# Modulation by VectorE: a two-layer hybrid recurrent block in which all but the first third of adaLN leaves TensorE's matmuls

## The chip, the cores and the metric

One core of a Trainium2 chip runs the whole kernel in one launch. The metric is the device time in microseconds; lower is better.

## The reference

Two layers work on 256 context tokens and 1024 latent tokens of 1024 channels. Each layer has a mixing sub-layer with four head groups (HGRN2, mLSTM, retention, GLA) and a squared-ReLU MLP. What matters here is adaLN: per layer, two conditioning vectors (context and latent) are each multiplied by a 1024 x 6144 matrix, and the six pieces of the result shift, scale and gate the two sub-layers.

```python
for layer in range(DEPTH):
    mod_l = (jax.nn.silu(c) @ w_ada[layer] + b_ada[layer])[:, None, :]
    mod_c = (jax.nn.silu(c_ctx) @ w_ada[layer] + b_ada[layer])[None, None, :]
    sh1_l, sc1_l, g1_l, sh2_l, sc2_l, g2_l = jnp.split(mod_l, 6, axis=-1)
    ...
    pl = split_proj(modulate(xl, sh1_l, sc1_l) @ w_in[layer])
    ...
    xl = xl + g1_l * mixer_out(raw_l, pl, g_heads[layer], w_out[layer])
    ...
    xl = xl + g2_l * sq_relu_mlp(modulate(xl, sh2_l, sc2_l), w_ff1[layer], w_ff2[layer])
```

where `modulate(x, shift, scale)` is `rmsnorm(x) * (1.0 + scale) + shift`. In the last layer the context's rows are needed by the mixers alone: its gates and its MLP are computed for the latent tokens only.

## The kernel before

Activations lie channel by token: eight channel tiles of 128 partitions, 1280 tokens in blocks of 256, 512 and 512. Each dense product takes three TensorE passes over split operands (lines 295 to 297, `mm3`; 569, and 600 to 602 for the two projections with tokens on the partitions). Weights arrive by DMA on SP's queue, ScalarE makes the high part (L283) and VectorE the rest (L284).

**Modulation.** The weights of a layer are cut into three thirds r (of 2048 columns) and eight channel tiles k. `ada_unit(l, r, k)` loads four pieces of 128 x 512 (L373) and multiplies each by the conditioning, 32 columns of which two are used, into 32 partitions of one PSUM bank (L374); the bank sums over k. After eight units `ada_finish` copies the bank (L380), transposes it (L383), adds the bias (L387) and, for scales, one (L391). Layer 0's first third comes ahead of everything. Its other two thirds (16 units) stand among the mLSTM's work, through four buffers; layer 1's three thirds (24 units) stand in layer 0's MLP, one after each feature tile, through two buffers.

**Mixers.** For each head group a generator emits steps and yields an estimated cost; `Fill` emits parts of dense projections between the steps, in proportion to the cost. Where `fill.also` is set, every eighth part also emits one modulation unit. The order of the groups is GLA, HGRN2 (two pairs of heads), mLSTM (two), retention (two). A feature tile is twelve parts (three token blocks by four), a projection with tokens on the partitions twenty. HGRN2's steps are many small VectorE operations (L851 to L1006, the multiply of queries at L959, short products L924, L968, L987); the mLSTM's are at L1265 to L1345.

**MLP.** A turn takes two feature tiles: first product (24 matmuls for each of three token blocks into a bank, ScalarE at L471 and L472, VectorE at L473 and L474), after each tile a call of `filler()`, then the second product (six matmuls a bank), which VectorE adds into the residual (L494). Layer 0 has 16 turns over 1280 tokens.

The instructions are traced in this order; a list scheduler of the framework places them on the engines' queues by its own estimates, so an instruction may stand somewhat before or behind its traced place. Every engine runs its queue in order. Eight scratch buffers of 512 words (`tmps`) serve the MLP.

Of the kernel before, what the change touches and what calls it, by code (L numbers as in the profile page):

```python
# [15 lines left out]
NK = 8  # L16
# [8 lines left out]
# constant arrays, by shape alone: name -> words  # L25
CONSTS = [("ones32", 32), ("ones", 128), ("sel", 128), ("ident", 128), ("bones", 128), ("m64", 512), ("lmask", 160),
          ("mlmask", 256), ("hsel", 8), ("eps", 1)]
# small per-call parameters
PARAMS = [("cc", 256), ("bada", 96), ("gfin", 8), ("ghead", 16), ("lblog", 8), ("mlb", 4), ("glb", 4), ("rtl", 24)]

# T-layout feature tiles of w_in
# [22 lines left out]
class Buf:  # L54
    """n words a partition of a tile"""
# [19 lines left out]
class Heap:  # L75
    """Places buffers in a few tiles at trace time; reuse waits by the bytes touched."""
# [13 lines left out]
    def top(self, n):  # L90
        """from the end of the first tile, or of what is free"""
        i, o, m = max((f for f in self.free_list if f[2] >= n), key=lambda f: (f[0] == 0, f[0], f[1]))
        self.free_list.remove((i, o, m))
        if m > n:
            self.free_list.append((i, o, m - n))
        b = Buf(self.tiles[i].t, o + m - n, n)
        b.i = i
        return b

    def alloc(self, n, low=False):  # L100
        """next fit; first fit for what lives long"""
# [14 lines left out]
    def free_head(self, n, *bufs):  # L116
        """the first words of buffers that are done with"""
# [21 lines left out]
class Dense:  # L139
    """a projection: its weights in n halves, then the products in small parts"""  # L140
# [16 lines left out]
class Fill:  # L157
    """dense work in small parts, traced between the steps of a mixer; the next weights ahead"""
# [9 lines left out]
    def step(self):  # L168
        while self.q:
# [3 lines left out]
            for cost in gen:  # L173
                self.n += 1
                if self.also and self.n % 8 == 0:
                    for c in self.also:
                        cost += c
                        break
# [9 lines left out]
    def along(self, gen, ratio, mark=10 ** 9):  # L188
        """a mixer, with this work, up to the mark, between its steps"""
# [10 lines left out]
class K:  # L200
# [19 lines left out]
    # ------------------------------------------------------------------ memory  # L220
# [4 lines left out]
    def pool(self, name, sizes, side="left"):  # L225
        """a pool of one tile for each size"""
# [49 lines left out]
    # ------------------------------------------------------------------ dense helpers  # L276
    def whalf(self, src, b, slot, eng=None):
        """512 words a partition of weights as (hi, lo), [128, 512 / b, b]"""
# [9 lines left out]
    def wtile(self, src, ring, eng=None):  # L288
        """a [1024, 128] tile of weights: k -> (hi, lo)"""
# [12 lines left out]
    def logsig(self, out, z, tmp, bias=None, scale=1.0):  # L302
        """tmp = ln(1 + exp(-|z + bias|)); out = min(z, 0) - tmp when no bias"""
# [13 lines left out]
    # ------------------------------------------------------------------ small parameters  # L317
# [8 lines left out]
    def params2(self, tmp):  # L326
        """hgrn lower bounds of layer 1, retention log decays"""
# [22 lines left out]
        # retention: log sigmoid(z) = min(z, 0) - 2 atanh(u / (2 + u)), u = exp(-|z|)  # L350
# [17 lines left out]
    # ------------------------------------------------------------------ ada  # L368
# [24 lines left out]
    # ------------------------------------------------------------------ norms  # L393
    def rstd(self, tb, fast=False):
        """1 / rms by token on every partition; fast: the squares summed by matrix products only"""
# [30 lines left out]
    def norm_mod(self, l, tbs, sh, sc):  # L426
        """modulated norm, block by block; the next block's statistics ahead"""
# [27 lines left out]
    # ------------------------------------------------------------------ MLP  # L455
    def mlp(self, l, tbs, wring, aring, filler, first, after):
        """first: weights of the first tiles; after: what follows the last sum of a token block"""
# [50 lines left out]
    def final_block(self, tb):  # L508
        """the statistics of this block, then the norm of the block before it"""
# [5 lines left out]
    # ------------------------------------------------------------------ projections  # L515
# [7 lines left out]
    def reserve(self, S, names, keep):  # L523
        """buffers for later work, apart from what the work before it takes"""
# [7 lines left out]
    def denseT(self, tile, tbs, evac):  # L532
        """a tile of features by channels"""
# [14 lines left out]
    def denseVS(self, S, sp):  # L548
        """v of GLA with the decay inputs and the gates of mLSTM, 304 columns, in [token, channel] layout"""
# [27 lines left out]
    def turn(self, sp):  # L577
        """these inputs and gates in [channel, token] layout"""
# [1138 lines left out]
```

## Time and profile before

| | us |
|---|---|
| median of three runs | 3391.35 |
| lowest and highest | 3391.2, 3393.93 |
| span of the profiled execution | 3386.0 |
| TensorE busy in it (matmul) | 3308.9 |
| VectorE busy | 1957.8 |
| ScalarE busy | 1284.9 |

The span runs from the first to the last instruction; no other time is given for the profiled execution. Ends of matmuls are modelled, and a matmul's row lasts longer than its distance from the next, so starts are what to compare. On a line of the timeline "x4" merges neighbours; an fp32 product gives two records.

### The profile page before, as it was taken

How to read it: one execution, taken by the hardware profiler on the slowest of the kernel's cores; microseconds unless marked ns; L12 is line 12 of the kernel's file. 1: busy time of each engine (PE TensorE's matmuls, PEld its weight loads, DVE VectorE, ACT ScalarE, POOL GpSimd, SP SyncE). 2: the span in 40 equal slices, each digit the busy share in tenths (PEclk: the TensorE clock that was granted, in tenths of full speed). 3: DMA queues.
4: the chain of work that ended last, by engine and by line, in shares of the span. 5: the costliest groups of instructions: out<-in, count | busy, mean ns of one | idle time of the engine just before them, and what ended most of it. 6: DMA issues, size and time to landing. Idle time of an engine off the chain costs nothing.

```text
span 3386.0 us, 52462 instructions
## 1 busy us (share of the span) xinstructions
PE 3308.9 (98%) x21020; PEld 2620.0 (77%) x21020; DVE 1957.8 (58%) x3806; ACT 1284.9 (38%) x2670; POOL 10.9 (0%) x41
## 2 busy tenths in 40 slices
PE   7999999999999999999999999999999999999998
PEld 4787876778877777777788688788777788888887
DVE  4878675646554444444445567866765655555556
ACT  4667663435321121121121456865534322222223
POOL 0000000000000000000000000000000000000000
PEclk9999999999999999999999999999999999999999
DMA  5223336526122222222111212333315111111111
GB/s 201 69 65 105 109 101 185 154 68 204 34 80 72 60 69 72 60 66 74 54 38 38 84 38 69 118 109 117 104 61 162 50 45 50 50 50 50 47 47 66
DMA packets 165790, 278.83 MB, mean 82 GB/s; under 512 B 20072, under 2 KB 49416, under 8 KB 165288
## 3 DMA queue, kind: packets, MB, share of 16 engines
q1 hardware_dynamic: 164248, 273.65, 26.1%
q8 instruction: 165, 2.70, 0.3%
q10 hardware_dynamic: 1296, 1.81, 0.2%
q14 instruction: 81, 0.66, 0.1%
HBM read 229.75 MB, written 45.64 MB: 81 GB/s over the span
## 4 chain that ended last, share of the span: by engine, by line
PE 85%; DMA 6%; DVE 4%; ACT 3%; issue 1%; SPq 0%; ACTq 0%; DVEq 0%
PE psum L295 21%; PE psum L296 21%; PE psum L297 21%; PE psum L374 3%; DMA pc<-w_ada 2%; PE psum L799 2%; PE psum L569 2%; PE psum L600 2%; PE psum L602 1%; PE psum L601 1%; PE psum L786 1%; PE psum L802 1%; PE psum L987 1%; PE psum L674 1%; PE psum L1326 1%
## 5 line engine op out<-in xcount | busy, mean ns | idle before, releaser
L494 DVE SCALAR_TENSOR_TENSOR x<-psum,st,x 128x512 f32<-128x512 f32 (+1 forms) x648 | 442.2, 690 | 274.9 <-PE psum L297 274.2
L283 ACT ACTIVATE pc<-st 128x512 fp32r<-128x512 f32 x256 | 161.1, 632 | 878.9 <-PE psum L296 866.7
L295 PE MATMUL psum<-pc,pc 128*128 128x512 f32 (+1 forms) x1296 | 478.1, 369 | 0.0
L296 PE MATMUL psum<-pc,pc 128*128 128x512 f32 (+1 forms) x1296 | 475.8, 367 | 0.0
L295 PE MATMUL psum<-Hhi,pc 128*128 128x512 f32 (+1 forms) x1280 | 473.8, 370 | 1.5 <-ACT pc L283 1.5
L297 PE MATMUL psum<-pc,pc 128*128 128x512 f32 (+1 forms) x1296 | 475.3, 367 | 0.0
L296 PE MATMUL psum<-Hlo,pc 128*128 128x512 f32 (+1 forms) x1280 | 473.2, 370 | 0.0
L297 PE MATMUL psum<-Hhi,pc 128*128 128x512 f32 (+1 forms) x1280 | 470.9, 368 | 0.0
L295 PE MATMUL psum<-Hhi,pw 128*128 128x512 f32 (+1 forms) x1192 | 448.5, 376 | 0.7 <-ACT pw L283 0.7
L297 PE MATMUL psum<-Hhi,pw 128*128 128x512 f32 (+1 forms) x1192 | 443.9, 372 | 0.0
L296 PE MATMUL psum<-Hlo,pw 128*128 128x512 f32 (+1 forms) x1192 | 443.5, 372 | 0.0
L473 DVE TENSOR_TENSOR st<-st 128x256 f32<-128x256 f32 (+1 forms) x160 | 101.9, 638 | 397.1 <-ACT pc L472 396.9
L295 PEld LDWEIGHTS psum<-pc,pc 128*128 128x128 f32 x1296 | 244.2, 188 | 63.2 <-issue 12.0
L295 PEld LDWEIGHTS psum<-Hhi,pc 128*128 128x128 f32 x1280 | 241.3, 188 | 63.3 <-ACT pc L283 11.6
L297 PEld LDWEIGHTS psum<-pc,pc 128*128 128x128 f32 x1296 | 243.9, 188 | 53.0 <-issue 12.8
L296 PEld LDWEIGHTS psum<-Hlo,pc 128*128 128x128 f32 x1280 | 241.2, 188 | 49.8 <-issue 9.7
L284 DVE TENSOR_TENSOR pc<-st,pc 128x512 fp32r<-128x512 f32 x256 | 176.2, 690 | 173.6 <-ACT pc L283 151.5
L296 PEld LDWEIGHTS psum<-pc,pc 128*128 128x128 f32 x1296 | 244.3, 189 | 40.7 <-issue 2.1
L297 PEld LDWEIGHTS psum<-Hhi,pc 128*128 128x128 f32 x1280 | 241.1, 188 | 41.0 <-DVE pc L284 0.6
L295 PEld LDWEIGHTS psum<-Hhi,pw 128*128 128x128 f32 x1192 | 225.4, 189 | 51.0 <-issue 14.9
L297 PEld LDWEIGHTS psum<-Hhi,pw 128*128 128x128 f32 x1192 | 225.3, 189 | 41.0 <-issue 5.8
L296 PEld LDWEIGHTS psum<-Hlo,pw 128*128 128x128 f32 x1192 | 225.5, 189 | 37.6 <-issue 3.8
(418 smaller groups left out, 4810.7 us busy)
## 6 DMA issues: line engine op xcount, KB each, us to landing
st<-w_ff SPq DMA_DIRECT2D x256, 256.0 KB
st<-w_inT SPq DMA_DIRECT2D x96, 256.0 KB
pc<-w_ada SPq DMA_DIRECT2D x96, 256.0 KB
ph<-w_ada SPq DMA_DIRECT2D x64, 256.0 KB
st<-w_out SPq DMA_DIRECT2D x50, 256.0 KB
d_z<-st SPq DMA_DIRECT2D x40, 256.0 KB
ps<-w_ada SPq DMA_DIRECT2D x32, 256.0 KB
x<-xT SPq DMA_DIRECT2D x32, 256.0 KB
```

Of the source, the lines that this page charges most:

```text
L283: nc.scalar.activation(hi, raw, AF.Copy)
L284: (eng or nc.vector).tensor_tensor(lo, raw, F(hi), op=ALU.subtract)
L295: t.matmul(out, lhsT=w[0], rhs=m[0], start=first, stop=False)
L296: t.matmul(out, lhsT=w[0], rhs=m[1], start=False, stop=False)
L297: t.matmul(out, lhsT=w[1], rhs=m[0], start=False, stop=last)
L374: nc.tensor.matmul(self.bank(bank)[32 * g:32 * g + 32, :], lhsT=self.cc[:, k, :], rhs=w, start=(k == 0), stop=(k == NK - 1), tile_position ...
L473: nc.vector.tensor_tensor(r, r, r, op=ALU.mult)
L494: nc.vector.scalar_tensor_tensor(x, ps, self.mod[:, l, 40 + o, j:j + 1], x, op0=ALU.mult, op1=ALU.add)
L569: t.matmul(ps[:, 0:304], lhsT=h[a], rhs=u[b], start=(k + i == 0), stop=(k == NK - 1 and i == 2))
L600: t.matmul(ps[:, e, :], lhsT=h[0], rhs=u[0], start=(k == 0), stop=False)
L601: t.matmul(ps[:, e, :], lhsT=h[0], rhs=u[1], start=False, stop=False)
L799: nc.tensor.matmul(o, lhsT=ST[r0:r0 + kd, c, d, :], rhs=qd[d](c)[r0:r0 + kd, :], start=(j == 0), stop=False, tile_position=(r0, 0))
```

## The change

The first third of layer 0 stays as it is. All other thirds are made by a new function `ada_part`. It takes W columns at a time (256 in layer 0, 512 in layer 1). For each of the eight channel tiles it loads 128 x W weights and, for each conditioning that is wanted, VectorE multiplies them by the conditioning's value on each partition and adds them to an accumulator in SBUF. After the eighth, TensorE multiplies each 128 columns of an accumulator by one column of ones, which sums over partitions and leaves the result in the wanted layout; VectorE adds the bias. Layer 0 takes both conditionings. Layer 1 takes both for its first third and the latent one alone for the rest.

In layer 0 this now starts ahead of HGRN2 and goes on through the mixers: on parts 0, 2 and 4 of every five, one step (a load with its operations, or a sum), with no cost counted against the part; 144 steps in all. Its six buffers of 256 words are held from there to the mixers' end; the sums take a bank of the dense ring, which keeps its three banks in the mLSTM. In layer 0's MLP each call of `filler()` takes four steps (108 in all). Four scratch buffers leave the MLP's ring: two join the two load buffers, two are accumulators. Comments are removed as well; that part of the diff is left out.

```diff
@@ Fill.step
-                if self.also and self.n % 8 == 0:
-                    for c in self.also:
-                        cost += c
-                        break
+                if self.also and self.n % 5 in (0, 2, 4):
+                    next(self.also, None)
@@ new
+    def ada_part(self, l, r, toks, wring, tmp, acc, banks, W):
+        nc = self.nc
+        one = self.m64[:, 1:2]
+        nt, nb = len(toks), W // 128
+        for q in range(2048 // W):
+            g, h = divmod(q * W, 512)
+            A = [b(W) for b in acc[:nt]]
+            for k in range(NK):
+                w = wring.next()(W)
+                nc.sync.dma_start(w, self.io["w_ada"][l, r, k, :, g, h:h + W])
+                for i, j in enumerate(toks):
+                    c = self.cc[:, k, j:j + 1]
+                    if k == 0:
+                        nc.vector.tensor_scalar(A[i], w, c, None, op0=ALU.mult)
+                    else:
+                        nc.vector.scalar_tensor_tensor(A[i], w, c, A[i], op0=ALU.mult, op1=ALU.add)
+                yield
+            ps = self.bank(banks().next())
+            for i in range(nt):
+                for cb in range(nb):
+                    nc.tensor.matmul(ps[:, 2 * cb + i:2 * cb + i + 1], lhsT=A[i][:, 128 * cb:128 * cb + 128], rhs=one,
+                                     start=True, stop=True)
...
+            nc.vector.tensor_tensor(mo, v, bb, op=ALU.add)
...
+            yield
@@ mixers, ahead of HGRN2
+        ao = hp.alloc(1536, True) if l == 0 else None
+        if l == 0:
+            fill.also = ada([ao.sub(256 * i, 256) for i in range(6)], lambda: self.dbanks)
@@ mixers, mLSTM
-        ao = hp.alloc(2048) if l == 0 else None
-        if l == 0:
-            self.dbanks = Ring((0, 1))
...
-                fill.also = ada(p, Ring([ao.sub(512 * i, 512) for i in range(4)]))
...
-                for _ in fill.also:
-                    pass
@@ build
-                    b.ada_unit(0, i + 1, k, 2, ring)
-                    yield 860
-                b.ada_finish(0, i + 1, 2, 2, b.tD.next())
+            for r in (1, 2):
+                yield from b.ada_part(0, r, (0, 1), Ring(bufs[:4]), None, bufs[4:6], banks, 256)
...
-            b.ada_unit(1, r, k, st["bk"], fring)
-            if k == 7:
-                b.ada_finish(1, r, st["bk"], b.banks.next(), b.tmps.next())
+                yield from b.ada_part(1, r, (0, 1) if r == 0 else (1,), Ring(bufs[:4]), None, bufs[4:6], lambda: b.banks, 512)
+        tmps = b.tmps
+        gen = ada1(cs[nw:nw + nf] + tmps.items[4:])
+        def filler():
+            for _ in range(4):
+                next(gen, None)
+        if l == 0:
+            b.tmps = Ring(tmps.items[:4])
```

## Rows read from the trace of the kernel before

**Rows 1.** The page: span, then busy time, share and instructions by engine.
```profile
span 3386.0 us, 52462 instructions
...
PE 3308.9 (98%) x21020; PEld 2620.0 (77%) x21020; DVE 1957.8 (58%) x3806; ACT 1284.9 (38%) x2670; POOL 10.9 (0%) x41
```

**Rows 2.** The page: the chain that ended last, share of the span by line.
```profile
PE psum L295 21%; PE psum L296 21%; PE psum L297 21%; PE psum L374 3%; DMA pc<-w_ada 2%; PE psum L799 2%; PE psum L569 2%; PE psum L600 2%; PE psum L602 1%; PE psum L601 1%; PE psum L786 1%; PE psum L802 1%; PE psum L987 1%; PE psum L674 1%; PE psum L1326 1%
```

**Rows 3.** Timeline of TensorE, layer 0's MLP: first matmuls of turns 1, 12, 15.
```profile
995.77 0.28 PE L295 MATMUL psum<-Hhi,pc 128*128 128x256 f32 x1
...
1696.49 0.28 PE L295 MATMUL psum<-Hhi,pc 128*128 128x256 f32 x1
...
1862.21 0.28 PE L295 MATMUL psum<-Hhi,pc 128*128 128x256 f32 x1
```

**Rows 4.** Timeline of TensorE around a modulation unit in the MLP.
```profile
963.41 1.05 PE L374 MATMUL psum<-pc,st 128*32 128x512 f32 x4
964.40 0.39 PE L295 MATMUL psum<-pc,pc 128*128 128x256 f32 x1
...
968.52 1.04 PE L374 MATMUL psum<-pc,st 128*32 128x512 f32 x2 [1.17 <-DMA pc<-w_ada]
```

**Rows 5.** Waits of TensorE: us in total, times, longest.
```profile
PE psum L374 <- DMA pc<-w_ada: 13.4, 23, 1.2
...
PE psum L374 <- DMA ph<-w_ada: 2.0, 3, 1.0
```

**Rows 6.** Windows, L374 alone: length, then busy us (records) of PE and PEld.
```profile
515.00:810.00 295.00, 42.65 (x128) 5.80 (x128) 1.00 0.47 141
...
925.00:1680.00 755.00, 76.48 (x192) 10.20 (x192) 1.00 0.24 67
```

**Rows 7.** Windows: busy PE, PEld, DVE, ACT, POOL; clock, DMA share, GB/s.
```profile
515.00:675.00 160.00, 156.95 (x1044) 108.89 (x1042) 97.32 (x262) 64.18 (x182) 0.39 (x3) 1.00 0.59 176
236.00:515.00 279.00, 273.62 (x2779) 222.45 (x2778) 207.23 (x493) 180.93 (x420) 1.20 (x11) 1.00 0.33 104
...
2360.00:2480.00 120.00, 115.87 (x858) 94.03 (x859) 90.01 (x233) 61.75 (x175) 0.31 (x2) 1.00 0.34 105
929.00:1697.00 768.00, 753.83 (x3669) 579.96 (x3668) 347.31 (x553) 147.09 (x258) 0.00 (x0) 1.00 0.23 67
```

**Rows 8.** Timeline of TensorE around a block of L924.
```profile
178.31 0.73 PE L924 MATMUL psum<-st,px 128*128 128x4 f32 x6
178.90 0.48 PE L297 MATMUL psum<-Hhi,pw 128*128 128x512 f32 x1
179.21 0.39 PE L295 MATMUL psum<-Hhi,pw 128*128 128x512 f32 x1
```

**Rows 9.** VectorE by line and form, 236 to 515: busy us, mean ns.
```profile
L959 DVE SCALAR_TENSOR_TENSOR px<-px,st 128x512 f32<-128x512 f32 x40 | 30.0, 750 | 6.9 <-ACT px L957 4.4 <-DMA px<-d_z 1.8
...
L959 DVE SCALAR_TENSOR_TENSOR px<-px,st 128x256 f32<-128x256 f32 x20 | 9.7, 485 | 2.2 <-ACT px L957 1.1
```

**Rows 10.** Windows with VectorE nearly full (columns of rows 7).
```profile
2040.00:2060.00 20.00, 18.15 (x257) 13.71 (x255) 19.06 (x41) 14.84 (x30) 0.00 (x0) 1.00 0.26 93
2180.00:2200.00 20.00, 20.00 (x177) 15.05 (x176) 18.05 (x40) 17.51 (x37) 0.00 (x0) 1.00 0.38 120
```

**Rows 11.** TensorE by line and form, 236 to 515: one dense pass of three.
```profile
L295 PE MATMUL psum<-Hhi,pw 128*128 128x512 f32 x160 | 64.2, 401 | 0.0
L600 PE MATMUL psum<-pw,Hhi 128*128 128x256 f32 x123 | 36.2, 295 | 0.4 <-ACT ph L728 0.4
L295 PE MATMUL psum<-Hhi,pw 128*128 128x256 f32 x79 | 22.8, 288 | 0.0
```

**Rows 12.** Waits of SP's queue: us in total, times, longest.
```profile
SPq L282 <- DVE pc L284: 1284.7, 223, 16.7
```

**Rows 13.** The chain in order of time: one load in the MLP.
```profile
964.49 3.99 DMA pc<-w_ada
```

More of the change, by code (lines that the diff above doesn't have):

```diff
@@ L391, in ada_finish @@
             nc.vector.tensor_scalar(m, m, 1.0, None, op0=ALU.add)
+    def ada_part(self, l, r, toks, wring, tmp, acc, banks, W):
[20 more added lines that the diff above has]
+                                     start=True, stop=True)
+            o = 16 * r + nb * q
+            mo = self.mod[:, l, o:o + nb, toks[0]:toks[0] + nt]
+            bb = self.bada[:, l, o:o + nb].unsqueeze(2).to_broadcast([128, nb, nt])
+            v = ps[:, 0:2 * nb].rearrange("p (c j) -> p c j", j=2)[:, :, 0:nt]
+            nc.vector.tensor_tensor(mo, v, bb, op=ALU.add)
+            if (r == 0 and g >= 2) or (r == 2 and g < 2):
+                nc.vector.tensor_scalar(mo, mo, 1.0, None, op0=ALU.add)
+            yield
     def rstd(self, tb, fast=False):
@@ L1442, in mixers @@
         self.rt_setup()
-        ao = hp.alloc(2048) if l == 0 else None
-        if l == 0:
-            self.dbanks = Ring((0, 1))
         for p in range(2):
-            if l == 0:
-                fill.also = ada(p, Ring([ao.sub(512 * i, 512) for i in range(4)]))
             self.fetch(ml[p], "K", MLK + p, TBS)
@@ L1458, in mixers @@
             fill.until(m)
-            if l == 0:
-                for _ in fill.also:
-                    pass
-                fill.also = None
-        if l == 0:
-            hp.free(ao)
-            self.dbanks = Ring((0, 1, 2))
         hp.free(ml[0]["V65"], self.mlN_o, self.mlAE_o)
@@ L1476, in mixers @@
         fill.until(10 ** 9)
+        if l == 0:
+            for _ in fill.also:
+                pass
+            hp.free(ao)
         for x in self.mix_pools:
@@ L1566, in build, with ada @@
         b.mix_open(l)
-        def ada(i, ring, l=l):
-            if l == 0:
-                for k in range(NK):
-                    b.ada_unit(0, i + 1, k, 2, ring)
-                    yield 860
-                b.ada_finish(0, i + 1, 2, 2, b.tD.next())
+        def ada(bufs, banks):
+            for r in (1, 2):
+                yield from b.ada_part(0, r, (0, 1), Ring(bufs[:4]), None, bufs[4:6], banks, 256)
         b.mixers(l, ada)
@@ L1579, in build, with ada1 @@
         pc, cs = b.pool(f"pc{l}", [1024] * nw + [512] * nf + [NT] * (2 * na))
-        wring, fring = Ring(cs[:nw]), Ring(cs[nw:nw + nf])
+        wring = Ring(cs[:nw])
         aring = Ring(zip(cs[nw + nf::2], cs[nw + nf + 1::2]))
-        st = {"i": 0, "bk": None}
-        def filler(l=l, st=st):
-            if l == 1 or st["i"] >= 24:
-                return
-            r, k = divmod(st["i"], 8)
-            if k == 0:
-                st["bk"] = b.banks.next()
-                b.banks.items.remove(st["bk"])
-            b.ada_unit(1, r, k, st["bk"], fring)
-            if k == 7:
-                b.ada_finish(1, r, st["bk"], b.banks.next(), b.tmps.next())
-                b.banks.items.append(st["bk"])
-            st["i"] += 1
+        def ada1(bufs, l=l):
+            for r in range(3) if l == 0 else ():
+                yield from b.ada_part(1, r, (0, 1) if r == 0 else (1,), Ring(bufs[:4]), None, bufs[4:6], lambda: b.banks, 512)
[4 more added lines that the diff above has]
+                next(gen, None)
+        if l == 0:
+            b.tmps = Ring(tmps.items[:4])
         first = [b.wtile(io["w_ff1"][l, f], wring) for f in range(2)]
@@ L1604, in build @@
         b.mlp(l, tbs, wring, aring, filler, first, after)
+        b.tmps = tmps
         pc.release()
```

## The prediction

> **What bounds the kernel now.** I read the page first, then the chain that ended last, then TensorE's timeline by turns of the MLP, then the engines by stage. The page says that TensorE's matmul rows cover nearly the whole span and VectorE's a little over half [rows 1]. The chain carries the point: after the dense products (L295 to L297) it names L374, the modulation products, with 3%, and the loads of their weights with 2% [rows 2]. So the modulation lies on the path; but the chain splits time between a load and the products beside it, so I price it by turns.
>
> Layer 0's MLP runs 16 turns of two feature tiles. Turn 1 starts at 995.77, turn 12 at 1696.49: 700.72 us for eleven turns with modulation units, 63.70 each. From 1696.49 to 1862.21 three turns without units take 55.24 each [rows 3]. Nothing else differs between them, so a turn with two units costs 8.46 us more. Inside, a block of L374 holds TensorE 0.99 us (963.41 to 964.40), and the third group of a unit comes after an idle 1.17 us behind its load, since two buffers serve four loads [rows 4]. Named waits for loads sum to only 13.4 us in the MLP [rows 5]: most of the price is execution.
>
> The other two thirds of layer 0 stand among the mLSTM's products: 128 records, 42.65 us busy, against 192 records and 76.48 us in the MLP [rows 6]. TensorE is busy for 156.95 of 160 us there, VectorE for 97.32; in the HGRN2 stage before it VectorE is busy for 207.23 of 279 [rows 7]. The granted clock reads 1.00 in all these windows, so no term comes from it.
>
> **The change, part by part.**
>
> *Removed in the MLP.* Twelve turns by 8.46 are 101.6 us, the loads' waits included.
>
> *Added there on TensorE.* Each sum over partitions is an fp32 product of 128 weight columns with one moving column. The nearest row is L924 (128 weight columns, 2 or 4 moving): six records, three products, from 178.31 to 178.90, so 0.20 each, and the dense product behind them takes 0.31 in place of 0.23 [rows 8]. A block of four costs 0.87 us, of eight 1.66. Layer 1 has four blocks of eight (first third, both conditionings) and eight of four (the rest, latent alone): 13.6 us.
>
> *Added there on VectorE.* 64 + 64 multiply-adds of 512 columns. The row for that form is L959's 750 ns [rows 9]: 96 us. VectorE then has 347.31 + 96 = 443 us in a stretch of 768 - 84 = 684 us [rows 7], 65%. I cost this at nothing. The cover is PSUM: a filler call puts at most eight multiply-adds (6.0 us) ahead of an accumulation out of PSUM, and a bank in the second product is filled by six matmuls of 0.23 us (1.4 us), so eight banks hold some 8 us or more in mixed widths. Without that cover all 96 us could show. The scratch ring that shrinks from eight to four buffers turns once in four chains of 24 products (5.4 us each); an ordinary chain of ACT and VectorE work needs less. Nothing.
>
> *Removed in the mLSTM.* Lower bound the bare 42.65; upper bound the MLP's ratio of price to busy time, 101.6/76.48 = 1.33, which gives 56.7. I take 46, near the lower: waits for loads here are 2.0 us [rows 5], and many blocks stand between other fp32 products, where no dense product pays for the switch. TensorE must find other work to gain it: the same stage of layer 1 has no modulation and TensorE is busy 115.87 of 120 us there, 96.6% against 98.1% [rows 7]. I add 2 us for that.
>
> *Added in layer 0's mixers on TensorE.* 16 blocks of four: 13.9 us.
>
> *Waits of these 28 blocks.* Each waits for the last multiply-add of its sum. Nothing to 0.58 us each (13.4/23, what an L374 block waits for a load [rows 5]): 0 to 16 us. I take 4, as blocks can be planned behind dense work.
>
> *Added in layer 0's mixers on VectorE.* Two thirds by eight pieces by eight channel tiles by two conditionings: 256 operations of 256 columns, 485 ns [rows 9], 124 us. One in eight is a plain multiply, which I price the same. They ride on three of five dense parts, from HGRN2's start. Up to 515 us some 151 of the 250 remaining parts run: L295's 160 + 79 products at 24 a tile are 10 tiles of 12 parts, and L600's 123 at 4 a part are 31 [rows 11]. So 90 steps fall there, 80 of them loads with two operations: 78 us. VectorE in HGRN2 becomes 207 + 78 = 285 us in a stage that TensorE alone would make 279 + 9 = 288 long: 99%. In the mLSTM it is 97 + 25 in about 160 - 37 + 3 = 126 us, 97%. So VectorE runs out of slack here. Below, the additions fit into its 72 idle microseconds and cost nothing; above, it keeps every idle moment it has now and the stage becomes 207 + 78 + 72 = 357, 69 us longer than 288. Rows near that load: at 18.05 of 20 us VectorE busy TensorE still reads 20.00, at 19.06 it reads 18.15 [rows 10]. A VectorE held to 95% makes HGRN2 300 us, 12 longer; I take 12 for both stages.
>
> The width is the one doubtful choice. A 256-column operation costs 485 ns and two of them 0.97 us, against 0.75 for one of 512 [rows 9]. [...]
>
> *Buffers and banks.* The loads hold 1536 words a partition from HGRN2 on, where 2048 were held in the mLSTM alone, and the mLSTM's dense products get three banks in place of two. No row prices either. TensorE's idle time, 5.4 of 279 us and 3.1 of 160 [rows 7], bounds what the third bank can win, and the words are under one slot and a half of the five that hold weights, so I take nothing for both.
>
> *Loads.* The bytes are the same, but 128 loads of half the width take the place of 64, now waiting on VectorE where they waited on TensorE. SP already stands long behind weight loads (1284.7 us in total [rows 12]), and a w_ada load takes 3.99 us on the chain [rows 13]. What is queued behind a waiting load are weights, fetches and spills. With four buffers each load can go three steps ahead (554 us / 144 steps = 3.8 us a step, 11 us ahead), so I cost it at nothing; the price if that fails is a rival below.
>
> **Sum** on the profiled execution's span: 3386.0 - 101.6 + 13.6 - 46 + 13.9 + 2 + 4 + 12 = 3283.9. The median of the runs, 3391.35, stands 5.35 above the span; with that, 3289 us.
>
> **The rivals.**
>
> *VectorE sets the pace of layer 0's mixers.* The term of 12 goes towards its bound of 69. For it: 99% and 97% above. Against: the dense parts still fill TensorE while a mixer is late. Time 3305 to 3346, the middle 3320. Chance 0.22.
>
> *The mLSTM's products were cover, not path.* Then its 46 us come back as waits of TensorE and only the MLP gains: 3335. Against: TensorE's 98% there, and 96.6% in layer 1. Chance 0.08. [...]
>
> *The change doesn't lighten TensorE.* If a sum costs what an L374 block costs whatever its width (0.97), 128 sums cost 124 us in place of 27: about 3386, no change. Against: L924's rows. Chance 0.03.
>
> *The other side: loads late on VectorE's own queue.* In VectorE's queue a multiply-add that waits for its load holds every evacuation and mixer step behind it. Half of 3.99 us for each of 128 loads is 255 us, with VectorE full: 3540. It turns slower than before from 102/128 = 0.8 us a load. For it: SP's long stands. Against: three steps of lead. Chance 0.04.
>
> **How the numbers follow.** The forecast above has 0.60 (3263 to 3310), still better 0.03 (down to 3261, with 56.7 removed in the mLSTM, no waits and no loss to VectorE). The range, 3263 to 3335, holds the forecast's own and most of the first rival. About 0.2% (7 us) is what a measurement of this kernel can tell from no change; so faster 0.92, same 0.03, slower 0.05.
>
> **What would show it.** L374 is left in the first 35 us alone. Turns of layer 0's MLP are all near 55.2 us plus 1.1 for sums, with no TensorE idle time named by VectorE's accumulations. From 236 us on VectorE's share rises above 95% until the mLSTM's end, while TensorE's stays over 96%, and retention starts some 10 to 25 us sooner. Wrong: if TensorE's idle time in the mixers grows by tens of us with VectorE named; if VectorE's own waits name w_ada; or if the blocks of sums take much over 0.2 us a product.

## The result, and the profile after

The changed kernel takes 3307.68 us (median of four executions, 3300.05 to 3315.91); the kernel before took 3391.49 beside it. The ratio is 0.975, 95% interval [0.9733, 0.9767]: faster by 2.5%. The forecast was 3289, the range 3263 to 3335. The profiled execution is the fastest of the four: 3300.05, span 3298.2, against 3386.0 before.

The page after, answering to [rows 1]:

```profile
span 3298.2 us, 52930 instructions
...
PE 3215.6 (97%) x20936; PEld 2640.0 (80%) x20936; DVE 2121.8 (64%) x4218; ACT 1286.1 (39%) x2665; POOL 10.8 (0%) x41
```

TensorE lost 93 us of busy rows and VectorE gained 164. To see where the span fell, use the marks of [rows 3]. L293 to L295 are now the dense products, L413 the sums over partitions. Timeline of TensorE after:

```profile
307.47 0.40 PE L295 MATMUL psum<-Hhi,pw 128*128 128x512 f32 x1
312.41 1.08 PE L1018 MATMUL psum<-px 128*32 128x64 f32 x32 [4.55 <-DVE px L990]
318.07 1.08 PE L1018 MATMUL psum<-px 128*32 128x64 f32 x32 [4.58 <-DVE px L990]
321.50 0.79 PE L293 MATMUL psum<-Hhi,pw 128*128 128x512 f32 x1 [2.35 <-DVE st L741]
322.09 0.63 PE L294 MATMUL psum<-Hlo,pw 128*128 128x512 f32 x1
322.52 0.63 PE L295 MATMUL psum<-Hhi,pw 128*128 128x512 f32 x1
...
991.43 0.28 PE L293 MATMUL psum<-Hhi,pc 128*128 128x256 f32 x1
...
1005.21 1.84 PE L413 MATMUL psum<-st 128*128 128x1 f32 x16
1006.91 0.37 PE L293 MATMUL psum<-Hhi,pc 128*128 128x256 f32 x1
...
1219.57 0.28 PE L293 MATMUL psum<-Hhi,pc 128*128 128x256 f32 x1
...
1723.92 0.28 PE L293 MATMUL psum<-Hhi,pc 128*128 128x256 f32 x1
...
1779.16 0.28 PE L293 MATMUL psum<-Hhi,pc 128*128 128x256 f32 x1
```

Read the lower half first. Turn 1 of layer 0's MLP starts at 991.43 (995.77 before), turn 15 at 1779.16 (1862.21 before). So the span's 87.8 us divide into 4.3 ahead of turn 1, 78.7 in turns 1 to 14, and 4.75 behind. Nearly all of it came in the MLP's turns; the 4.75 lie in layer 1, which the change doesn't touch, and are within chance (see ahead of experiment 1). The four turns from 991.43 to 1219.57 take 57.04 each, one without modulation still 55.24 (1723.92 to 1779.16). The 4.3 ahead of turn 1 hold turn 0's own gain, so the mixers, from which the forecast expected 16 us, gave nothing that one execution can tell. The upper half shows why: TensorE stood still for 4.55, 4.58 and 2.35 us, with VectorE named, and the products behind follow each other by 0.43 us (322.09 to 322.52) where the same form took 0.23 (1003.62 to 1003.85 in the same timeline).

The engines after, by stretch (columns of rows 7): HGRN2 from its start to the mLSTM's first product at 545.3 (before: 236 to 515), the mLSTM, the MLP's turns, and then, in slices of 20 us, the part of HGRN2 in which TensorE stands still most (called the hole below):

```profile
236.00:545.00 309.00, 282.08 (x2772) 227.75 (x2771) 260.90 (x655) 181.17 (x412) 1.28 (x12) 0.95 0.41 125
545.00:687.00 142.00, 140.19 (x1041) 118.57 (x1040) 111.97 (x316) 67.48 (x193) 0.24 (x2) 1.00 0.43 126
991.00:1697.00 706.00, 706.00 (x3738) 609.51 (x3737) 409.99 (x674) 145.17 (x257) 0.00 (x0) 1.00 0.23 70
...
290.00:310.00 20.00, 17.41 (x190) 13.21 (x188) 18.93 (x50) 16.45 (x43) 0.00 (x0) 1.00 0.26 84
310.00:330.00 20.00, 10.66 (x126) 8.64 (x127) 17.40 (x40) 7.41 (x14) 0.00 (x0) 0.66 0.26 86
```

HGRN2's stretch grew from 279 to 309 us. That length is not a loss by itself, since other dense parts run in it: run 9 below has no hole, and its mLSTM's first product still comes at 530.5. The idle time is: TensorE idles 26.9 us of it where it idled 5.4 [rows 7], and its granted clock has a mean of 0.95 where it was 1.00: between 310 and 330 it is 0.66, where the timeline has the idle times. In windows of half a microsecond it reads 1.00 up to 311.5, 0.50 from 312 to 325 (the lower level below) and 1.00 again from 325.5. VectorE is busy for 260.90 of 309, 84%, and not the 99% that the prediction worked out. The MLP's stretch shows the opposite: TensorE without any idle time.

What VectorE did while TensorE waited until 312.41 (timeline of VectorE after; L990 is L959 of before):

```profile
305.25 1.67 DVE L408 SCALAR_TENSOR_TENSOR ph<-ph,st 128x256 f32<-128x256 f32 x4
306.84 0.69 DVE L310 SCALAR_TENSOR_TENSOR st<-psum,st 128x512 f32<-128x512 f32 x1
...
308.78 0.68 DVE L722 TENSOR_TENSOR st<-st,psum 128x512 f32<-128x512 f32 x1
309.74 0.75 DVE L990 SCALAR_TENSOR_TENSOR px<-px,st 128x512 f32<-128x512 f32 x1 [0.28 <-ACT px L988]
310.40 1.22 DVE L731 TENSOR_TENSOR_SCAN st<-st 128x512 f32<-128x512 f32 x1
311.54 0.72 DVE L990 SCALAR_TENSOR_TENSOR px<-px,st 128x512 f32<-128x512 f32 x1
```

Four multiply-adds (1.59 us from start to start) and three operations of the dense work stand in the queue among the mixer's steps; the L990 that TensorE needs ends at 312.26. From 305.25 to 312.26 VectorE is idle for 0.28 us in all. No single operation is to blame. Each delays all that stands behind it in the queue, and TensorE's next product in its own queue needs this one result.

Two views answer the doubts about loads and sums. The multiply-adds themselves (operation of L408 in the mixers, count, ns, idle time ahead), and all of VectorE's waits for these loads in the mixers; then TensorE's waits from 236 to 900:

```profile
L408 DVE SCALAR_TENSOR_TENSOR ph<-ph,st 128x256 f32<-128x256 f32 x224 | 99.7, 479 | 0.2 <-DMA ph<-w_ada 0.2
```

```profile
PE psum L1018 <- DVE px L990: 10.1, 5, 4.6
...
PE psum L413 <- DVE ph L408: 3.5, 1, 3.5
```

VectorE waited 0.2 us for loads in 224 operations, and TensorE 3.5 us, once, for the last multiply-add of a sum. There is a wait the other way too, which the prediction doesn't have: the plain multiply that begins a sum (L406) waited 4.2 us, in two times, until TensorE had read the two accumulators. Its waits end at 714.7 and 740.3, not in the hole.

### The profile page after: what moved, and what is told of

Its sections match the earlier page's. It is cut to its first block, busy times and chain, and to the rows that moved or that the text cites. A ratio compares the mean times of both kernels' runs of the same rounds, so it can differ in the third digit from the quotient of the medians.

```text
span 3298.2 us, 52930 instructions
## 1 busy us (share of the span) xinstructions
PE 3215.6 (97%) x20936; PEld 2640.0 (80%) x20936; DVE 2121.8 (64%) x4218; ACT 1286.1 (39%) x2665; POOL 10.8 (0%) x41
## 4 chain that ended last, share of the span: by engine, by line
PE 88%; DVE 5%; DMA 3%; ACT 3%; issue 1%; SPq 0%; DVEq 0%; ACTq 0%
PE psum L293 23%; PE psum L294 23%; PE psum L295 23%; PE psum L830 2%; PE psum L600 2%; PE psum L631 2%; PE psum L633 2%; PE psum L632 1%; PE psum L817 1%; PE psum L833 1%; PE psum L1018 1%; PE psum L705 1%; PE psum L1357 1%; PE psum L413 1%; DVE px L990 1%
## 5 line engine op out<-in xcount | busy, mean ns | idle before, releaser
L293 PE MATMUL psum<-pc,pc 128*128 128x512 f32 (+1 forms) x1296 | 475.8, 367 | 0.0
L295 PE MATMUL psum<-pc,pc 128*128 128x512 f32 (+1 forms) x1296 | 473.8, 366 | 0.0
L293 PE MATMUL psum<-Hhi,pc 128*128 128x512 f32 (+1 forms) x1280 | 471.9, 369 | 1.7 <-ACT pc L281 1.5
L295 PE MATMUL psum<-Hhi,pc 128*128 128x512 f32 (+1 forms) x1280 | 470.5, 368 | 0.0
L293 PE MATMUL psum<-Hhi,pw 128*128 128x512 f32 (+1 forms) x1192 | 451.0, 379 | 5.7 <-ACT pw L281 2.5
L295 PE MATMUL psum<-Hhi,pw 128*128 128x512 f32 (+1 forms) x1192 | 445.2, 374 | 0.0
L293 PEld LDWEIGHTS psum<-pc,pc 128*128 128x128 f32 x1296 | 244.4, 189 | 43.8 <-DVE x L525 1.3
L295 PEld LDWEIGHTS psum<-pc,pc 128*128 128x128 f32 x1296 | 244.0, 188 | 43.0 <-issue 2.7
L293 PEld LDWEIGHTS psum<-Hhi,pc 128*128 128x128 f32 x1280 | 241.2, 189 | 43.5 <-ACT pc L281 2.4
L295 PEld LDWEIGHTS psum<-Hhi,pc 128*128 128x128 f32 x1280 | 241.1, 188 | 40.9 <-DVE pc L282 0.6
L293 PEld LDWEIGHTS psum<-Hhi,pw 128*128 128x128 f32 x1192 | 226.7, 190 | 51.4 <-issue 10.1
L295 PEld LDWEIGHTS psum<-Hhi,pw 128*128 128x128 f32 x1192 | 226.2, 190 | 37.6 <-issue 2.1
```

The costliest lines, as they stand in the source:

```text
L293: t.matmul(out, lhsT=w[0], rhs=m[0], start=first, stop=False)
L295: t.matmul(out, lhsT=w[1], rhs=m[0], start=False, stop=last)
```

## The experiments

"T1" below is the start of turn 1 in the profiled execution: it holds the mixers and turn 0 and nothing that follows. It is 995.77 before, 991.43 after.

How much of a T1 is chance? Layer 1's mixers, from turn 15 to the first product of layer 1's MLP, tell. No edit reaches them, and the counts of instructions agree to a record or two; yet this stretch takes from 799.57 us (run 11) to 809.66 (run 9), 803.17 after and 807.83 before. Run 11, then run 9, windows (columns of rows 7):

```profile
1778.81:2578.38 799.57, 780.51 (x6136) 625.93 (x6134) 542.35 (x1156) 441.32 (x947) 8.73 (x21) 1.00 0.29 93
...
1752.16:2561.82 809.66, 788.12 (x6136) 632.21 (x6134) 542.13 (x1156) 441.33 (x947) 8.75 (x21) 0.99 0.29 92
```

VectorE and ScalarE are busy as long in both; the granted clock is not the same (last section). So a difference of some us between two T1 is not read below, and up to 10 us may be chance; the medians and their intervals come first.

**1. The MLP's part alone.** Layer 0's other thirds stay L374 products in the mLSTM; the MLP is as changed.

```diff
-                if self.also and self.n % 5 in (0, 2, 4):
-                    next(self.also, None)
+                if self.also and self.n % 8 == 0:
+                    for c in self.also:
...
```

> The change in layer 0's MLP alone; layer 0's second and third thirds stay on TensorE in the mLSTM as before. By the profile after, turns of the MLP fell from 63.70 to 57.04 and 56.14 us, some 85 us over the twelve turns, and that is nearly all of the gain. So if the mixers' part of the change is worth nothing net (all theories of why agree on this), this kernel takes 3306 us, the same as the changed one within its spread. If the mixers' part had won what was forecast for it (16 us), it takes 3324 us. Its granted clock should be that of the kernel before, 0.996.

3298.14 us, ratio 0.9733 [0.9715, 0.9751], T1 987.22. The MLP is worth 2.7%, some 90 us; the mixers' part is worth nothing that can be measured (the intervals overlap, and the 4.2 us by which T1 is earlier without it may be chance). The T1 of this kernel stands 8.55 ahead of before, near the 8.46 of turn 0's products.

**2. The latent conditioning alone in layer 0** (the context's gates, shifts and scales are not computed: they take the latent ones).

```diff
-                yield from b.ada_part(0, r, (0, 1), Ring(bufs[:4]), None, bufs[4:6], banks, 256)
+                yield from b.ada_part(0, r, (1,), Ring(bufs[:4]), None, bufs[4:6], banks, 256)
...
```

> The changed kernel with layer 0's context conditioning left out of the multiply-adds and sums (the latent one's result is written to both columns, so part of the computation is left out): half of VectorE's added operations in layer 0's mixers go, 62 us in place of 124, and half of the sums on TensorE (7 us), while loads, steps, buffers and banks stay. Theory A (VectorE's queue is full in HGRN2's first pair, so that mixer steps and evacuations come late and TensorE stands, and its clock falls after): TensorE's hole between 300 and 400 us is mostly gone and the time is 3270 to 3285. Theory B (loads: SP's queue stands at w_ada loads that wait for VectorE, and dense weights behind them come late): some gain as VectorE frees buffers sooner, 3285 to 3300. Theory C (the 1536 words taken from the heap make its buffers wait): no gain but the 7 us of sums, 3293 to 3300.

3282.04 us, 0.9689 [0.9672, 0.9706], T1 967.31: half the multiply-adds and half the sums give back 24 us by T1, of which the sums are an estimated 7 (half of the prediction's 13.9). The hole is smaller: 17.22 of 20 us busy from 310 to 330 at a granted clock of 0.74, for 10.66 at 0.66.

**3. No loads** (layer 0's multiply-adds use what the first four loads brought; gates, shifts and scales are meaningless).

```diff
+                if l == 1 or (r == 1 and q == 0 and k < 4):
                     nc.sync.dma_start(w, self.io["w_ada"][l, r, k, :, g, h:h + W])
```

> The changed kernel with layer 0's loads left out but for the first four: every multiply-add and sum in the mixers runs as before on those four tiles (the weights of the others are left out). VectorE's work, the sums, buffers and steps stay; SP has 124 loads less to stand behind. Theory A: the hole between 300 and 400 us stays and the time is 3298 to 3310. Theory B: the hole goes and the time is 3272 to 3285. Theory C: as A.

3304.95 us, 0.9759 [0.9738, 0.9779], T1 993.25. The loads are not it: the windows of this kernel show the same hole.

```profile
310.00:330.00 20.00, 9.40 (x118) 7.91 (x119) 18.80 (x43) 7.45 (x14) 0.00 (x0) 0.57 0.21 71
```

**4. A later start**, behind the first HGRN2 pair, buffers and all, three parts in four.

```diff
         fill.until(m1)
+        ao = hp.alloc(1536, True) if l == 0 else None
+        if l == 0:
+            fill.also = ada([ao.sub(256 * i, 256) for i in range(6)], lambda: self.dbanks)
         self.feat_hg(hg[1])
...
```

> The changed kernel with the steps of layer 0 started one stage later, behind HGRN2's first pair of heads and the evacuations of the second pair's decays, at three of every four dense parts in place of three of five, so that they still end ahead of the output projection. The same operations, loads and sums. Theory A: the stretch in which VectorE has both those evacuations and HGRN2's own steps is spared; TensorE's hole shrinks and the time is 3275 to 3292; VectorE's share after 380 us rises to 90 to 95%. Theory B and C: the same standing of SP and the same heap only later, 3298 to 3310.

3349.96 us, 0.9889 [0.9872, 0.9907], T1 1039.12: far worse, against every theory in hand. In one window neither TensorE nor VectorE was busy for much over half:

```profile
380.00:420.00 40.00, 20.89 (x157) 13.53 (x158) 19.34 (x61) 16.74 (x46) 0.10 (x1) 0.50 0.24 75
```

The first multiply-add runs at 417.5, so this hole is not their work. SP stood 15.1 us at L755, a fetch of the second pair, until VectorE's L931 had let go of its buffer: buffers taken in another order moved the second pair's, which is the likely cause. Two more kernels were to part the place of the work from that of the buffers.

**5. The same later start with the buffers taken where the change takes them**, three parts in five.

```diff
         ao = hp.alloc(1536, True) if l == 0 else None
-        if l == 0:
-            fill.also = ada([ao.sub(256 * i, 256) for i in range(6)], lambda: self.dbanks)
...
         fill.until(m1)
+        if l == 0:
+            fill.also = ada([ao.sub(256 * i, 256) for i in range(6)], lambda: self.dbanks)
```

> The 1536 words are taken where the changed kernel takes them, ahead of the first HGRN2 pair, but the multiply-adds start only behind that pair, at the changed kernel's rate. A (VectorE's queue is too full in the first HGRN2 pair, which idles TensorE and lowers its clock): the hole from 300 to 400 us goes, 3272 to 3290 us. C (the words withheld from the heap make the hole, and misplaced them again in the run before that started late): the hole stays, 3295 us or more. If both fall and the multiply-adds behind the pair make a new hole, 3295 us or more with the first pair at full pace.

3313.47 us, 0.9778 [0.9762, 0.9794], T1 1002.53: 36 us better than run 4, no better than the change. But the edit did not move the work as it meant to. The scheduler placed the multiply-adds far ahead of their traced place: their first operation runs at 281.9 (279.8 in the change), and in the first pair's stretch (its last L990 ends at 412 here, 414 in the change) stand 51 of them, against 61 in the change. Windows of L408 alone (length, busy us of VectorE with records, clock, DMA), this run and then the change:

```profile
281.00:412.00 131.00, 23.17 (x51) 0.93 0.39 126
...
281.00:412.00 131.00, 27.39 (x61) 0.88 0.37 114
```

So the first pair was not spared, and the 36 us against run 4 are the buffers' order, the rate and the work's place together. The windows of all engines show a smaller hole in the first pair and others later:

```profile
300.00:340.00 40.00, 34.80 (x342) 28.10 (x340) 36.15 (x78) 27.59 (x55) 0.00 (x0) 0.90 0.27 90
...
600.00:640.00 40.00, 37.51 (x220) 31.77 (x220) 25.85 (x77) 12.72 (x40) 0.00 (x0) 0.72 0.32 101
680.00:720.00 40.00, 34.91 (x231) 25.88 (x230) 32.38 (x84) 14.66 (x35) 0.00 (x0) 0.87 0.32 102
800.00:840.00 40.00, 30.11 (x162) 27.05 (x161) 30.31 (x63) 18.36 (x32) 0.00 (x0) 0.83 0.72 233
```

The last is of this kernel's making: at this rate 16 steps were left at the mixers' end, and TensorE waited 9.2 us for their sum. The others are not. None of the expectation's three cases was put to the test, since each takes the first pair as free of the work; the later holes show that it is not the only place where the work costs.

**6. The buffers alone**: run 1 with 1536 words withheld in HGRN2.

```diff
+        held = hp.alloc(1536, True) if l == 0 else None
         self.feat_hg(hg[0])
...
+        if l == 0:
+            hp.free(held)
```

> The kernel with the MLP's part alone (3298.1 us), with 1536 words withheld from the heap through HGRN2 and no other edit. A: TensorE keeps its pace in HGRN2, within 4 us of 3298. C: a hole between 290 and 400 us, 3308 us or more.

3291.6 us, 0.9718 [0.9701, 0.9735], T1 984.77. Withheld words cost nothing at the change's place.

**7. 512 columns in layer 0.**

```diff
-                yield from b.ada_part(0, r, (0, 1), Ring(bufs[:4]), None, bufs[4:6], banks, 256)
+                yield from b.ada_part(0, r, (0, 1), Ring(bufs[:2]), None, bufs[2:4], banks, 512)
...
```

> Layer 0's multiply-adds 512 columns wide in place of 256: half the instructions, 2 load and 2 sum buffers of 512 words (2048 withheld in place of 1536), three steps in ten in place of six. By the MLP's 512-wide rows (0.75 us each) they occupy VectorE 112 x 0.75 = 84 us in place of about 100. A: a smaller hole by the share of the work that goes, 3295 to 3305 us. C: more words withheld, a larger hole, 3310 us or more.

3302.21 us, 0.9742 [0.9727, 0.9756], T1 989.80: not to be told from the change. (Two load buffers have the place of four; VectorE waited 2.5 us for loads.) The greater width, which the prediction left in doubt, shows no gain here that can be measured. From start to start a 256-column multiply-add takes 0.40 us (four in 1.59), and a 512-column one of L990 0.64 (311.54 to L732 at 312.18), so two narrow ones cost 0.16 more than a wide one, not the 0.22 that the rows' durations gave.

**8. GpSimd in VectorE's place**, a product and an addition for each multiply-add, one part in two.

```diff
-                        nc.vector.scalar_tensor_tensor(A[i], w, c, A[i], op0=ALU.mult, op1=ALU.add)
+                            nc.gpsimd.tensor_scalar(tmp(W), w, c, None, op0=ALU.mult)
+                            nc.gpsimd.tensor_tensor(A[i], A[i], tmp(W), op=ALU.add)
...
```

> Layer 0's multiply-adds on GpSimd, each as a product and an addition (256 columns), 3 load buffers in place of 4 and the one freed for the product; one step in two in place of three in five. A: VectorE's queue in HGRN2 is as before the change, TensorE keeps its pace, and the mixers' part gives what the prediction's sum had without contention, about 46 - 14 - 2 = 30 us: 3268 to 3285 us. If GpSimd's work slows VectorE's, or the loads wait for GpSimd on SP's queue, it is 3295 us or more, and the waits of TensorE or SP name which.

3473.93 us, 1.0254 [1.0239, 1.0269], T1 1160.31: slower than before. GpSimd's groups by form, and SP's waits from 236 to 1130:

```profile
L411 POOL TENSOR_SCALAR ph<-ph,st 128x256 f32<-128x256 f32 x224 | 239.6, 1070 | 21.6
L412 POOL TENSOR_TENSOR ph<-ph 128x256 f32<-128x256 f32 x224 | 180.7, 807 | 17.4
```

```profile
SPq L402 <- POOL ph L411: 336.4, 105, 5.7
```

1.9 us for what VectorE does in 0.48. SP stands behind it for 336 us with every other load in its queue. That is the standing which the prediction's part on loads costed at nothing, here with GpSimd; the fourth rival's, a multiply-add that waits for its load, is another one. So the run says nothing for or against VectorE's share.

**9. No multiply-adds but the first of each block in layer 0.**

```diff
-                    else:
+                    elif l:
                         nc.vector.scalar_tensor_tensor(A[i], w, c, A[i], op0=ALU.mult, op1=ALU.add)
```

> Layer 0's multiply-adds but the first of each block are left out (so gates, shifts and scales of its second and third part are not the reference's); its loads, its sums over partitions and its places in the program stay. The time between this kernel and the changed one is what those 224 instructions cost on VectorE. Prediction's sum: 12 us, 3295 us. Theory L (VectorE's load alone makes the hole and the fall of the clock, in whichever part of the mixers it stands): the hole at 300 to 400 us goes, 3262 to 3276 us. If the loads or the sums on TensorE cost as much, it stays within 8 us of the changed kernel.

3277.84 us, 0.9668 [0.9651, 0.9686], T1 964.43. The 224 instructions cost 27.0 us by T1, 29.8 by the medians. The windows of this kernel:

```profile
236.00:545.00 309.00, 298.28 (x2966) 242.61 (x2965) 221.39 (x547) 185.82 (x433) 1.29 (x12) 0.99 0.47 150
...
310.00:330.00 20.00, 18.31 (x188) 14.53 (x192) 17.48 (x39) 12.25 (x24) 0.00 (x0) 0.91 0.71 227
```

The hole is gone, loads and sums and buffers being the same. What the 27 us are made of shows from 236 to 960, in the change and then in this run, and in the change's three stretches at the lower level:

```profile
236.00:960.00 724.00, 688.81 (x5351) 563.28 (x5350) 558.53 (x1329) 369.81 (x844) 1.53 (x14) 0.98 0.39 120
311.90:325.40 13.50, 6.06 (x75) 5.06 (x76) 12.67 (x30) 4.37 (x8) 0.00 (x0) 0.50 0.39 126
359.60:366.20 6.60, 6.60 (x59) 6.42 (x59) 6.01 (x14) 3.01 (x6) 0.00 (x0) 0.50 0.30 97
383.50:393.50 10.00, 7.01 (x34) 5.04 (x33) 6.90 (x17) 4.65 (x10) 0.00 (x0) 0.50 0.60 185
...
236.00:960.00 724.00, 708.76 (x5490) 582.18 (x5490) 500.14 (x1139) 370.94 (x850) 1.53 (x14) 0.99 0.39 122
```

TensorE idles 35.2 us in the change and 15.2 here: 20 of the 27. At the lower level it is busy for 19.7 us in the change, which at full clock would be an estimated 9.8 less. This run has three such stretches too, busy in all of their 9.6 us, an estimated 4.8. So some 5 us are the clock, and 2 are left. The low level is cheaper than its share of the time suggests, because TensorE stood still in a third of it.

**10. The multiply-adds spread from GLA's mixing on**, four parts in nine.

```diff
-                if self.also and self.n % 5 in (0, 2, 4):
+                if self.also and self.n % 9 in (0, 2, 4, 6):
...
         hp.free(sp["sp"])
+        ao = [hp.alloc(256, True) for _ in range(6)] if l == 0 else None
+        if l == 0:
+            fill.also = ada(ao, lambda: self.dbanks)
...
```

> The same multiply-adds spread from GLA's mixing on, four steps in nine in place of three in five, in six buffers of 256 words. L: the hole in HGRN2 shrinks with the rate (0.44 for 0.6) and by more than it grows in GLA: 3282 to 3297 us. If the place does not matter but each multiply-add costs the same wherever it is put, within 5 us of the changed kernel.

3289.89 us, 0.9703 [0.9686, 0.9719], T1 978.30. The interval lies below the change's: 13 of the 27 us come back by T1 (16 by the ratios), with every multiply-add in the program. Over the same stretch VectorE is nearly as busy as after the change (260.90 there), and TensorE is not held up:

```profile
236.00:545.00 309.00, 299.17 (x3061) 243.82 (x3058) 256.57 (x648) 190.17 (x435) 1.35 (x12) 0.99 0.38 119
```

So VectorE's busy time in a stretch does not decide. What does is not parted by this run. Three things differ from the change: what the multiply-adds stand in front of, their number here (108 of L408 against 135, as some ran in GLA), and six buffers taken one by one in place of one block. Windows of L408 alone, this run and then the change:

```profile
236.00:545.00 309.00, 48.48 (x108) 0.99 0.38 119
...
236.00:545.00 309.00, 60.26 (x135) 0.95 0.41 125
```

**11. One third each**: layer 0's second third on VectorE at three parts in ten, the last as L374 products in the mLSTM.

```diff
-                if self.also and self.n % 5 in (0, 2, 4):
+                if self.also and self.n % 10 in (0, 3, 6):
...
-            for r in (1, 2):
+            for r in (1,):
```

> Layer 0's second part (shift, scale, gate of the mixers' output) on VectorE at three steps in ten, its third part on TensorE in mLSTM as before the change, with two load buffers; the MLP's part as changed. L: half of the load, spread over the same stretch, costs little, while TensorE still loses half of the products: 3298 - 23 + 7 + 1 = 3283, range 3277 to 3292 us, ahead of the kernel with the MLP's part alone. If each multiply-add costs what it saves, 3296 to 3303 us.

3297.9 us, 0.9735 [0.9716, 0.9754], T1 991.08: no better than run 1, the second case of the expectation. Even at half the rate (41 of L408 from 281 to 412, where the change has 61 and run 10 has 48) the first HGRN2 pair shows a hole, so the number alone does not decide either:

```profile
280.00:320.00 40.00, 33.35 (x327) 26.42 (x326) 36.39 (x88) 29.34 (x72) 0.00 (x0) 0.87 0.33 108
```

**12. As run 10, with none in the first HGRN2 pair** and five parts in nine behind it.

```diff
-                if self.also and self.n % 9 in (0, 2, 4, 6):
+                if self.also and (self.n % 9 in (0, 2, 4, 6) if self.n < 80 else self.n >= 117 and self.n % 9 in (0, 2, 4, 6, 8)):
```

> As the run spread from GLA's mixing on (3289.9 us), but with no multiply-add during the first HGRN2 pair, where VectorE is fullest without them, and five steps in nine behind it. L with the place deciding: the 8 us that TensorE idles from 280 to 400 us in that run go, 3276 to 3287 us. If the higher rate behind it costs as much (the run that started behind the pair showed holes between 560 and 720 us), 3288 to 3300 us.

3303.78 us, 0.9743 [0.973, 0.9757], T1 998.18: worse than run 10 by 14 us. But the first pair was not free of them here either: none run from 236 to 334, and then 42 of L408 stand in the pair's mixing, before its last L990 ends at 431. Run 10 has 32 in the like stretch, 326 to 424.

```profile
322.00:431.00 109.00, 19.15 (x42) 0.85 0.37 116
```

So the pair got more of the work at once, and whether sparing it would help is not shown. The windows of all engines show where the time went:

```profile
360.00:400.00 40.00, 31.52 (x261) 23.14 (x262) 30.46 (x70) 17.25 (x34) 0.26 (x2) 0.66 0.26 86
...
680.00:720.00 40.00, 34.65 (x236) 28.98 (x235) 35.27 (x100) 18.86 (x55) 0.00 (x0) 0.79 0.38 116
```

In the first VectorE is not full (30.46 of 40), though 17 of L408 stand there; TensorE's largest named wait there is 2.8 us, for ScalarE's L687. In the second it is 5.0 us, for VectorE's L1134.

## Why the prediction came out as it did

- **The MLP: right.** Forecast -101.6, +13.6 and its share of the waits; eleven turns would give 79 us, and turns 1 to 14 gave 78.7. A block of eight products takes 1.70 us from start to start (1005.21 to 1006.91), forecast 1.66 from L924. VectorE's multiply-adds, 96 us by the forecast, were free: TensorE is busy in every microsecond of 991 to 1697, and a turn is longer than one without modulation by 1.80 us where it has a block of eight and by 0.90 where it has one of four. That the PSUM banks are the cover was not tried by itself. Run 1 holds this part alone.
- **Taking the products out of the mLSTM: near the forecast.** -46 + 13.9 + 2 and some 2 for waits is -28; run 9, which has this without the multiply-adds, stands at T1 22.8 ahead of run 1. The second rival (the products were cover) would have it near nothing and falls. The 5 us between are within the chance of a T1.
- **The step that failed in size is the contention on VectorE: 12 us, where run 9 shows 27.** It ate all that the mLSTM gave. Some 20 of the 27 are idle time of TensorE and some 5 the clock. The first rival named the mechanism, VectorE holding TensorE up in the mixers, and its bounds (0 to 69) held the value, but its picture was not right either. The step compared busy sums with the stage's length, found 99%, and took an engine that is full as the condition. VectorE was busy at 84% of HGRN2, the row's 485 ns being 0.40 from start to start, and TensorE was held up all the same: it waited 4.55 us for an L990 that stood in VectorE's queue behind other work. Run 10, with 256.57 us of VectorE's time busy in the stretch for 260.90 and no such hole, shows that the sum of busy time was the wrong measure.
- **"No term comes from it", of the clock, was wrong.** The clock read 1.00 in the windows before, where no wait of TensorE that is named from 236 to 810 is longer than 1.0 us. The change itself made the idle times at which the level fell; by run 9 that is some 5 us.
- **Loads, buffers, sums: right at about nothing.** 0.2 us of waits for loads in the mixers, run 3 without loads no faster beyond its interval, run 6 with words withheld not slower, 3.5 us of waits for sums in the mixers for 4 in all. Run 4 suggests that buffers cost where their order changes, which no run parts from the rest.
- **What the views should have shown:** the old products (L374, now L372) only up to 33.1 us, as forecast; layer 0's MLP turns as forecast (57.04 and then near 56); VectorE's share over 95% and TensorE's over 96% in HGRN2 both failed (84% and 91%); retention's first product came 11.3 us later (671.1 before, 682.4 after) and not 10 to 25 sooner; of the sign of a wrong forecast, TensorE idle by tens of us with VectorE named, a part came.

Put together, by the starts of turn 15: -87.3 for the MLP (run 1: 8.55 in T1 and 78.7 in turns), -22.8 for the mLSTM's products (run 9 against run 1), +27.0 for the multiply-adds (the change against run 9) make -83.1, where the forecast's terms make -86, -28 and +12, so -102. The other 4.75 of the profiled execution's -87.8 lie in layer 1's mixers, within their spread. The median lies a further 7.6 above the profiled execution, whose mean clock was the highest of the four.

The range held, and 3307.68 lies near the upper end of the forecast's own band (3263 to 3310). It lies in the first rival's (3305 to 3346) as well, so the number alone doesn't tell the two apart; run 9 does, and it speaks for the rival's mechanism.

What stays open: why one placing costs 27 us and another 13 less. Run 10 excludes VectorE's busy time in the stretch, run 11 the number of multiply-adds alone, and the later holes of runs 5 and 12 show that the first HGRN2 pair is not the only place. That the order in VectorE's queue decides is the likeliest reading and is not shown: runs 5 and 12 were to move the work out of the first pair, and in the traces it stands there still. No run set the order by hand, and none parts it from the buffers' order. Of the kernels that compute everything, runs 6 and 10 came out fastest; their intervals overlap, so that the mixers' part is worth anything is shown by none.

## What to carry to other kernels

Work moved from a bound engine to one with idle time was free where the receiving engine's results had slack (here the MLP, 96 us at no cost), and dear where the bound engine takes each result at once from the same ordered queue (here the mixers, 27 us for 100). After moving work in a program that a scheduler orders, look in the trace for where it went, as two runs here did not test what they were built for. Look at what stands behind the moved work in the queue and who waits for it, before adding up busy time; and where TensorE might newly stand still, price the clock as well (here it read 0.50 by the end of the 4.55 us, and cost some 5 us by run 9). Try the two stages apart: the kernel with the good half alone was no slower than the whole change.

## What the runs showed of the hardware

With TensorE idle for 4.55, 4.58 and 2.35 us the granted clock fell to 0.66 as a mean over 20 us, and 512-column products came 0.43 us apart in place of 0.23. Run 5 shows the level low over a stretch in which TensorE's rows are nearly unbroken: busy for 37.51 of 40 us at 0.72. It fell there among short products with idle times of 1.07 and 1.99 us.

The same idle time does not always cost the same. In layer 1's mixers TensorE stands still for 2.78 us, for the same result of VectorE, in run 11 and in run 9:

```profile
1871.91 0.51 PE L604 MATMUL psum<-pw,Hhi 128*128 128x304 f32 x2 [2.78 <-DVE ph L608]
1872.26 0.30 PE L604 MATMUL psum<-pw,Hlo 128*128 128x304 f32 x1
...
1845.65 0.85 PE L600 MATMUL psum<-pw,Hhi 128*128 128x304 f32 x2 [2.78 <-DVE ph L604]
1846.30 0.46 PE L600 MATMUL psum<-pw,Hlo 128*128 128x304 f32 x1
```

Behind it two products take 0.35 us in run 11, where the clock reads 1.00 from 1870 to 1890, and 0.65 in run 9, where it reads 0.83 from 1844 to 1854.

One kernel's times differ along with its mean clock. The four executions after are 3300.05, 3303.15, 3312.2 and 3315.91 us at mean clocks of 0.992, 0.989, 0.988 and 0.986, in the same order. The kernel before spreads too: beside runs 9 to 11 its seven executions lie between 3383.89 us at 0.997 and 3396.7 at 0.993.
